# A two-layer decoder trunk on one core: the FFN's down projection by a seven-product scheme, with weight sums made by adding DMA

## The chip, the cores and the metric

The kernel runs on one core of one Trainium2 chip. The metric is the device time of one execution in microseconds (us). Three runs of the kernel before took 1354.49, 1356.29 and 1356.95 us; the median is 1356.29 us.

## The reference, cut to what matters

```python
D_MODEL, SEQ, DEPTH, D_FF = 1024, 512, 2, 2816
def reference(x, ...):
    for l in range(DEPTH):
        proj = x @ w_in[l]
        ...
        mix = jnp.concatenate([o_a, o_b], axis=-1) @ w_out[l]
        x = layer_norm(ALPHA * x + mix, ln1_g[l], ln1_b[l])
        ffn = (jax.nn.silu(x @ w_ffn_gate[l]) * (x @ w_ffn_up[l])) @ w_ffn_down[l]
        x = layer_norm(ALPHA * x + ffn, ln2_g[l], ln2_b[l])
    return x
```

Everything is float32. The change is in the line of `ffn`: three matrix products per layer, 512 x 1024 by 1024 x 2816 twice (gate and up), and 512 x 2816 by 2816 x 1024 (down).

## The kernel before, in words

**Precision.** A float32 product is made of three products in the type fp32r. Each operand is split into a high part (a cast on ScalarE, ACT) and a low part (a subtraction on VectorE, DVE); `mm3` (L78) then issues high x high (L80), low x high and high x low (L81, L82), 128 x 128 stationary elements each, with 256 or 512 moving columns. A weight block of 128 x 1024 comes by DMA from the queue of SyncE (SP) into a raw buffer `wraw`, and is split into `whi` and `wlo` (`load_w`, L53; the cast is L74, the subtraction L75). Raw buffers have the tag `wr` with two buffers, `whi` and `wlo` have three each.

**Gate and up.** The inner layer has 22 blocks of 128 (NF). The first four blocks of gate and of up are plain (`feats`, L176): the first five of these eight products run in two halves of 256 tokens (the list `LEAD2`), the other three with 512 columns. The other 18 blocks go through `seven` (L122), Strassen's scheme in Winograd's form, two blocks (one unit) at a time: seven products of 4 x 3 matmuls with 256 columns each, where plain blocks need eight. Its sums of weights are made in `stage` (L92): `s1` and `s3` are loaded by SP and then added to by a DMA of GpSimd's queue with `accum_op=add` (L100, L101), 128 x 512 elements each. The sums of activations, T1 to T4, are made once per layer (L934 to L942). `seven` computes 18 units per layer.

**Down.** `H[j]`, the hidden block j, is split into high and low (`split_h` L948, `split_rest` L1030). The output has two halves of 512 columns (c = 0, 1) and four tiles of 128 tokens (t). For c = 0, eleven weight blocks (`down_w`, L1051, each 2 x 128 rows by 512 columns) are multiplied for all four t (`wide_mm`, L215); for c = 1 the tiles 0 and 1 come first, then their normalization runs (`norm_turn`, L719, or in the last layer `norm`, L709) beside the products of the tiles 2 and 3. That makes 22 x 4 x 2 x 3 = 528 matmuls of 512 columns per layer. None of the down weights is summed.

**Order.** A scheduler of the framework sets each engine's order when the program is built; every engine and every DMA queue then works in its order. `tc.high_priority(offset)` moves instructions ahead in that order. Buffers are named by tags with a fixed number of buffers; a tile waits until an earlier one of its tag is free.

Of the kernel before, what the change touches and what calls it, by code (L numbers as in the profile page):

```python
# [13 lines left out]
OP = mybir.AluOpType  # L14
# [5 lines left out]
LEAD1 = (("f", 3), None, None, None, ("at", 8))  # L20
LEAD2 = (None, None, ("qs", 6), ("e", 4), ("pt", 4))
# [13 lines left out]
class Kern:  # L35
# [17 lines left out]
    def load_w(self, src, w=1024, tag=None, pieces=1):  # L53
# [5 lines left out]
        if tag is None:  # L59
            hi = [self.sb.tile([128, 1024], F32R, name="whi", tag="wh", bufs=3)]  # L60
            lo = [self.sb.tile([128, 1024], F32R, name="wlo", tag="wl", bufs=3)]
            step = 1024
        elif tag == "a":
            b = self.big("wa", F32R).rearrange("p a b -> p (a b)")
            hi, lo, step = [b[:, :1024]], [b[:, 1024:]], 1024
        else:
            step = w // (1 if tag[0] == "f" else 2)
            hi, lo = ([self.sb.tile([128, 1024 if tag[0] == "f" else 512], F32R, name="wx", tag=tag[0], bufs=tag[1])
                       for _ in range(w // step)] for _ in range(2))
# [52 lines left out]
    def seven(self, units, R):  # L122
# [4 lines left out]
        self.place = 0  # L127
# [8 lines left out]
        for unit in units + [None]:  # L136
# [211 lines left out]
    def hg_levels(self, h, tag):  # L348
# [7 lines left out]
        dg = self.sb.tile([128, 4, 128], F32, name="atd", tag="at", bufs=8)  # L356
        M = self.sb.tile([128, 2, 128], F32, name="atm", tag="a7", bufs=6)
        a7 = self.sb.tile([128, 2, 128], F32, name="at7", tag="a7", bufs=6)
        a8 = self.sb.tile([128, 2, 256], F32, name="at8", tag="at", bufs=8)
# [111 lines left out]
    def take_q(self, u, pt):  # L471
        nc = self.nc
        for i in range(2):
            q = self.sb.tile([128, 512], F32R, name="qs", tag="qs", bufs=6)
# [17 lines left out]
    def compress(self, l, kind, pt, sp):  # L492
# [13 lines left out]
        for half in range(2):  # L506
            for j in range(8):
                if j % 4 == 0:
                    w1 = self.sb.tile([128, 512], F32, name="w1", tag="pt", bufs=4)
                    nc.sync.dma_start(w1, self.io["w1"][l, kind, half][:, j * 128:(j + 4) * 128])  # L510
                nc.tensor.matmul(ph[:, :62], w1[:, j % 4 * 128:(j % 4 + 1) * 128], U[half][:, j].rearrange("p g n -> p (g n)"),
# [67 lines left out]
    def nsa_scores(self, h, b):  # L579
# [7 lines left out]
        e1 = self.sb.tile([128, 512], F32, name="e1", tag="e", bufs=4)  # L587
        e2 = self.sb.tile([128, 256], F32, name="e2", tag="e2", bufs=2)
        e3 = self.sb.tile([128, 512], F32, name="e3", tag="e", bufs=4)
# [37 lines left out]
    def nsa_pv(self, h, b):  # L627
# [6 lines left out]
        for js in ((0,), (1,), (2, 3)):  # L634
# [6 lines left out]
            ph = self.sb.tile([128, 512], F32R, name="pth", tag="pt", bufs=4)  # L641
            pl = self.sb.tile([128, 512], F32R, name="ptl", tag="pt", bufs=4)
# [66 lines left out]
    def norm(self, t, r, p, res):  # L709
# [5 lines left out]
        for c in range(0, 1024, n):  # L715
            nc.vector.scalar_tensor_tensor(r[:, c:c + n], r[:, c:c + n], rs, p[:, 1024 + c:1024 + c + n], op0=OP.mult, op1=OP.add)
            nc.sync.dma_start(res[t * 128:(t + 1) * 128, c:c + n], r[:, c:c + n])
# [35 lines left out]
    def layer(self, l):  # L753
# [44 lines left out]
        if l == 0:  # L798
# [5 lines left out]
              for k0, k1, t in ((0, 3, None), (3, 6, None), (6, 8, ("qs", 6)))]  # L804
# [79 lines left out]
        def second_half():  # L884

            self.stats = [self.small(24, "st", tag="s") for _ in range(NT)]
            self.wo = [self.load_w(io["wo"][l, q, 0], tag=t) for q, t in enumerate((("at", 8), ("at", 8), ("f", 3), None))]
# [56 lines left out]
        NE = 6  # L944
        slots = [self.sb.tile([128, 512], F32R, name="h_" + tag, tag=tag, bufs=n) for tag, n in (("at", 8),) for _ in range(n)]
        H = [None] * NF

        def split_h(j, s):  # L948
            hh, hl = slots[2 * j], slots[2 * j + 1]
            with tc.high_priority(offset=500):  # L950
                nc.scalar.copy(hh, s)
                nc.vector.tensor_tensor(hl, s, hh.bitcast(F32), op=OP.subtract)
            H[j] = [(hh[:, b * 256:(b + 1) * 256], hl[:, b * 256:(b + 1) * 256]) for b in range(2)]

        pend = {}

        def ffn(i, pt):
            if i % 2 == 0:
                s = self.m([128, 512], "silu")
                with tc.high_priority(offset=500):  # L960
                    nc.scalar.activation(s, pt, AF.Silu)
                pend[0] = s
            else:
                s = pend.pop(0)
                with tc.high_priority(offset=500):
                    nc.vector.tensor_tensor(s, pt, s, op=OP.mult)
                split_h(i // 2, s)
# [5 lines left out]
        slots += [self.sb.tile([128, 512], F32R, name="h_pt", tag="pt", bufs=4) for _ in range(4)]  # L973
        raws = {}

        def hidden(j):

            if j < NE:
                return self.m([128, 512], "silu")
            if j - NE < 10:  # L980
                tag, n = (("qs", 6), ("e", 4))[j - NE >= 6]
                return self.sb.tile([128, 512], F32, name="h_" + tag, tag=tag, bufs=n)
            if j % 2 == 0:
                raws["f"] = self.sb.tile([128, 2, 512], F32, name="h_f", tag="f", bufs=3)
            return raws["f"][:, j % 2]

        def gate(j):
            def take(part, acc, add):
                if part == "11":
# [206 lines left out]
```

## Time and profile before

| | |
|---|---|
| runs | 1354.49, 1356.29, 1356.95 us |
| profiled execution | 1357.27 us, span of its instructions 1355.5 us |
| TensorE (PE) busy | 1322.2 us, 98% |
| DVE, ACT, GpSimd (POOL) busy | 938.9, 718.5, 158.6 us |
| granted TensorE clock | 0.996 of full speed |
| DMA | 170.26 MB, mean 126 GB/s |
| FFN of layer 0 | from about 327 us to about 681 us |
| FFN of layer 1 | from about 996 us to about 1344 us |

A matmul row's duration includes its way through a pipeline; the rate is read from the distance of the starts of consecutive rows. The span ends about 1.8 us before the execution's own time does.

### The profile page before, as it was taken

The numbers are of one execution on the slowest core, as the hardware profiler recorded it, in microseconds if no ns is written. First come the engines' busy times: TensorE is split into PE (matmuls) and PEld (weight loads), VectorE is DVE, ScalarE is ACT, GpSimd is POOL, SyncE is SP. The second block draws the span as 40 slices with busy tenths as digits, with TensorE's granted clock in tenths as the row PEclk, the third lists the DMA queues.
The fourth block names the chain that finished last, engine by engine and source line by source line (L and its number), as shares of the span: only waits on it lengthen the run. The fifth ranks groups of instructions, "written<-read, shape, count | busy, mean of one in ns | idle before, by whom it ended". The sixth has DMA issues, their size and how long they took to land.

```text
span 1355.5 us, 23189 instructions
## 1 busy us (share of the span) xinstructions
PE 1322.2 (98%) x8853; PEld 1212.5 (89%) x8853; DVE 938.9 (69%) x1914; ACT 718.5 (53%) x1460; POOL 158.6 (12%) x232
## 2 busy tenths in 40 slices
PE   8999999899999999999999999998999999999996
PEld 6988999789999999888899989987899999998885
DVE  4755898866887777624469468988559777775355
ACT  5254777745565555522543558778265655564131
POOL 1140111110011111000011001111000211100001
PEclk9999999999999999999999999999999999999999
DMA  7252213252177776334534122132513787754344
GB/s 235 79 164 101 78 56 101 55 146 91 63 174 191 180 182 171 102 107 151 191 122 129 65 86 75 55 106 73 154 47 102 181 192 181 181 131 140 94 143 152
DMA packets 61775, 170.26 MB, mean 126 GB/s; under 512 B 7519, under 2 KB 7695, under 8 KB 61152
## 3 DMA queue, kind: packets, MB, share of 16 engines
q1 hardware_dynamic: 44928, 128.93, 29.9%
q0 software_dynamic: 15728, 38.02, 13.4%
q10 hardware_dynamic: 1008, 1.84, 0.4%
q8 instruction: 69, 1.13, 0.3%
q14 instruction: 42, 0.34, 0.1%
HBM read 164.51 MB, written 7.10 MB: 127 GB/s over the span
## 4 chain that ended last, share of the span: by engine, by line
PE 88%; ACT 4%; DMA 3%; DVE 3%; issue 1%; POOL 0%; POOLq 0%; DVEq 0%; ACTq 0%; SPq 0%
PE ps_d L80 16%; PE ps_d L81 15%; PE ps_d L82 15%; PE ps_t L81 4%; PE ps_t L82 4%; PE ps_t L80 4%; PE ps_s L82 4%; PE ps_s L81 4%; PE ps_s L80 4%; PE ps_t L639 2%; DMA wraw<-in_wo 2%; PE ps_h L384 1%; PE ps_o L650 1%; PE ps_o L82 1%; PE ps_o L81 1%; PE ps_o L80 1%
## 5 line engine op out<-in xcount | busy, mean ns | idle before, releaser
L75 DVE TENSOR_TENSOR wlo<-wraw,whi 128x1024 fp32r<-128x1024 f32 (+1 forms) x122 | 149.0, 1221 | 158.2 <-ACT whi L74 157.7
L74 ACT CAST whi<-wraw 128x1024 fp32r<-128x1024 f32 (+1 forms) x122 | 127.5, 1045 | 227.4 <-PE ps_t L82 70.1
L80 PE MATMUL ps_d<-xh,whi 128*128 128x512 f32 (+1 forms) x456 | 154.1, 341 | 3.1 <-ACT gates L490 2.9
L112 ACT CAST whi<-wraw 128x512 fp32r<-128x512 f32 x144 | 89.0, 621 | 124.3 <-PE ps_d L81 93.9
L82 PE MATMUL ps_d<-xh,wlo 128*128 128x512 f32 (+1 forms) x456 | 154.6, 340 | 0.0
L81 PE MATMUL ps_d<-xl,whi 128*128 128x512 f32 (+1 forms) x456 | 154.2, 339 | 0.0
L113 DVE TENSOR_TENSOR wlo<-wraw,whi 128x512 fp32r<-128x512 f32 x144 | 98.4, 689 | 43.4 <-ACT whi L112 39.7
L81 PE MATMUL ps_d<-tl,whi 128*128 128x256 f32 x432 | 121.5, 283 | 0.0
L82 PE MATMUL ps_d<-th,wlo 128*128 128x256 f32 x432 | 120.5, 283 | 0.0
L80 PE MATMUL ps_d<-th,whi 128*128 128x256 f32 x432 | 120.3, 283 | 0.0
L80 PEld LDWEIGHTS ps_d<-xh,whi 128*128 128x128 f32 x456 | 85.8, 190 | 12.3 <-ACT gates L490 3.3
L82 PEld LDWEIGHTS ps_d<-xh,wlo 128*128 128x128 f32 x456 | 86.5, 190 | 8.8
L81 PEld LDWEIGHTS ps_d<-xl,whi 128*128 128x128 f32 x456 | 86.5, 190 | 8.3
L80 PE MATMUL ps_d<-whi,xh 128*128 128x256 f32 (+1 forms) x304 | 90.2, 298 | 0.0
L81 PE MATMUL ps_d<-wlo,xh 128*128 128x256 f32 (+1 forms) x304 | 88.4, 291 | 0.0
L82 PE MATMUL ps_d<-whi,xl 128*128 128x256 f32 (+1 forms) x304 | 87.3, 288 | 0.0
L81 PEld LDWEIGHTS ps_d<-tl,whi 128*128 128x128 f32 x432 | 82.9, 192 | 0.2
L80 PEld LDWEIGHTS ps_d<-th,whi 128*128 128x128 f32 x432 | 82.2, 192 | 0.2
L82 PEld LDWEIGHTS ps_d<-th,wlo 128*128 128x128 f32 x432 | 82.3, 192 | 0.0
L600 ACT ACTIVATE e<-e,mn 128x128 f32<-128x128 f32 (+3 forms) x128 | 71.6, 560 | 13.2 <-DVE mn L598 12.6
L598 DVE CUSTOM_DVE_ANT_0 e<-ps_s,strip 128x128 f32<-128x128 f32 (+3 forms) x128 | 59.2, 484 | 6.8 <-PE ps_s L613 5.9
L643 ACT CAST pth<-ps_t 128x384 fp32r<-128x384 f32 (+1 forms) x96 | 48.8, 510 | 25.9 <-PE ps_t L639 20.8
(482 smaller groups left out, 3957.7 us busy)
## 6 DMA issues: line engine op xcount, KB each, us to landing
wraw<-in_wd SPq DMA_DIRECT2D x59, 512.0 KB, 3.5
wraw<-in_wf SPq DMA_DIRECT2D x31, 512.0 KB, 3.3
wraw<-in_wg SPq DMA_DIRECT2D x26, 512.0 KB, 4.5
wraw<-in_wu SPq DMA_DIRECT2D x26, 512.0 KB, 4.1
ws<-in_wg SPq DMA_DIRECT2D x36, 256.0 KB, 3.5
ws<-in_wg POOLq DMA_DIRECT2D x36, 256.0 KB, 5.2
ws<-in_wu SPq DMA_DIRECT2D x36, 256.0 KB, 3.4
ws<-in_wu POOLq DMA_DIRECT2D x36, 256.0 KB, 4.6
```

The costliest lines, as they stand in the source:

```text
L74: nc.scalar.copy(h, raw[:, i:i + n])
L75: nc.vector.tensor_tensor(o, raw[:, i:i + n], h.bitcast(F32), op=OP.subtract)
L80: first = t.matmul(out, ah, bh, start=start, stop=False, **kw)
L81: t.matmul(out, ah, bl, start=False, stop=False, **kw)
L82: t.matmul(out, al, bh, start=False, stop=stop, **kw)
L112: nc.scalar.copy(h, raw)
L113: nc.vector.tensor_tensor(o, raw, h.bitcast(F32), op=OP.subtract)
L384: nc.tensor.matmul(p2[:, i], S[:, blk(i)], kq(128 * (i + 2), [[2 * w, n], [256 + w, 2], [1, w]]), start=True, stop=True)
L598: nc.vector.tensor_tensor_reduce(out=e, in0=pa, in1=st[:, 512 - pa.shape[-1]:], scale=1.0, scalar=3e38, op0=OP.add, op1=OP.min, accum_out=mn)
L600: nc.scalar.activation(e, e, AF.Exp, bias=mn, scale=-1.0, accum_out=sm)
L639: nc.tensor.transpose(p[:, c:c + 128], E[qt][:, j * 128:(j + 1) * 128], self.ident)
L643: nc.scalar.copy(ph[:, :c], p[:, :c])
```

## The change

It does four things.

1. Gate and up: two blocks each stay plain (all four in two halves of 256 columns, `LEAD2`), and twenty go through `seven` (20 units). Every third unit's raw block goes to the tag `f`. The rest of the first normalization (`norm_rest`) moves behind the third unit.
2. Down: 16 of 22 hidden blocks go through a seven-product scheme, in four groups q of four blocks, in two phases of four groups. In phase 1 a group has four products (called here M, Y, E and Z after their PSUM tiles), 2 x 2 x 3 = 12 matmuls of 512 columns each. M uses the weight block p11 as it is; Y, E and Z use one buffer `s` in which a sum grows: s is loaded by SP and added to once (`raw_w`) for Y, added to again for E, and again for Z. In phase 2 a group has three products (Q with a sum of two blocks, M and N with plain ones), and from the second group on one plain product.
3. The other six hidden blocks stay plain: 72 matmuls of 512 columns for the first tiles and 72 for the others, which come last, beside the normalization of the tiles 0 and 1.
4. Some pairs of 512-column buffers become one of 1024 columns, and in the last layer three of the output's stores go through GpSimd's queue.

The core of the diff (the merging of buffers and the drains into the rows are left out):

```diff
     def stage(self, sa, sb):
...
-            a = self.sb.tile([128, 1024], F32, name="wraw", tag="wr", bufs=2)
+            self.turn += 1
+            tag, bufs = ("f", 3) if self.turn % 3 == 0 else ("wr", 2)
+            a = self.sb.tile([128, 1024], F32, name="wraw", tag=tag, bufs=bufs)
...
-        srcs = [io[w][l, j] for j in range(4) for w in ("wg", "wu")]
-        self.feats(srcs[:5], x1, ffn, LEAD2)
-        self.norm_rest(l, 0, rows, None)
-        self.feats(srcs[5:], x1, lambda i, pt: ffn(i + 5, pt))
...
+        self.feats([io[w][l, j] for j in range(2) for w in ("wg", "wu")], x1, ffn, LEAD2)
...
-        self.seven([(io[w][l, j], io[w][l, j + 1], f(j)) for j in range(4, NF, 2) for w, f in (("wg", gate), ("wu", up))], R)
+        self.seven([(io[w][l, j], io[w][l, j + 1], f(j)) for j in range(2, NF, 2) for w, f in (("wg", gate), ("wu", up))], R,
+                   {3: lambda: self.norm_rest(l, 0, rows, None)})
...
-        for i in range(n):
-            for _ in range(min(len(rest), 4 if i == 0 else 2)):
-                split_rest(rest.pop(0))
-            self.wide_mm(pts, down_w(0, i), hsf, i, i == 0, i == n - 1, i == n - 1)
...
+        def split(dst, src):
+            with tc.high_priority(offset=3000):
+                nc.scalar.copy(dst[0], src)
+                nc.vector.tensor_tensor(dst[1], src, dst[0].bitcast(F32), op=OP.subtract)
...
+        def split_w(raw):
+            w = [self.sb.tile([128, 1024], F32R, name=nm, tag=t, bufs=3) for nm, t in (("whi", "wh"), ("wlo", "wl"))]
+            split(w, raw)
+            return w
+
+        def raw_w(src, plus=None, tag=("wr", 2)):
+            t = self.sb.tile([128, 1024], F32, name="wraw", tag=tag[0], bufs=tag[1])
+            nc.sync.dma_start(t, src)
+            if plus is not None:
+                nc.gpsimd.dma_start(t, plus, accum_op=OP.add)
+            return t
+
+        def dprod(acc, w, r, start, stop):
+            for k in range(2):
+                for t in range(2):
+                    s = slice(t * 128, (t + 1) * 128)
+                    self.mm3(acc[t], r[0][:, k, s], r[1][:, k, s], *(p[:, k * 512:(k + 1) * 512] for p in w),
+                             start and k == 0, stop and k == 1, skip_group_check=True)
...
+        for q in range(QS):
...
+            with tc.high_priority(offset=3000):
+                s = raw_w(wd[1, i], wd[1, i + 1], ("f", 3))
+                p11 = raw_w(wd[0, i])
...
+            dprod(M, split_w(p11), o11, q == 0, False)
+            dprod(Y, split_w(s), o1, q == 0, end)
+            with tc.high_priority(offset=3000):
+                nc.gpsimd.dma_start(s, wd[0, i], accum_op=OP.add)
+            dprod(E, split_w(s), o2, q == 0, end)
+            with tc.high_priority(offset=3000):
+                nc.gpsimd.dma_start(s, wd[0, i + 1], accum_op=OP.add)
+            dprod(Z, split_w(s), o22, q == 0, end)
...
+        for q in range(QS):
...
+            with tc.high_priority(offset=3000):
+                s3 = raw_w(wd[0, i], wd[1, i], ("f", 3))
+                p12, p22 = raw_w(wd[0, i + 1]), raw_w(wd[1, i + 1])
...
+            dprod(Q, split_w(s3), o3, q == 0, end)
+            dprod(M, split_w(p12), o21, False, False)
+            dprod(N, split_w(p22), o4, q == 0, end)
+            if q:
...
+                w1[j] = self.load_w(wd[0, j], tag=("at", 4) if q < 3 else ("pt", 2))
+                plain(M, j, (0, 1), w1[j], False, end)
```

In the changed kernel the cast of `split` is L1015, its subtraction L1016, the load in `raw_w` L1033 and its adding DMA L1035, the two later adding DMAs L1069 and L1072.

**Where the order changes, first place.** ScalarE in the down projection of layer 0, before: casts of down weights (`whi<-wraw`) and of hidden blocks (`hb`).

```order
L74 CAST whi_6448<-wraw_6446 128x1024
L74 CAST whi_6488<-wraw_6486 128x1024
L1039 CAST hb_6555<-h_f_5881 128x256 x2
L1039 CAST hb_6555<-h_f_6134 128x256 x2
L1039 CAST hb_6554<-h_f_6134 128x256
L74 CAST whi_6526<-wraw_6524 128x1024
L74 CAST whi_6566<-wraw_6564 128x1024
L74 CAST whi_6604<-wraw_6602 128x1024
L74 CAST whi_6634<-wraw_6632 128x1024
```

The same engine and place in the changed kernel: `wraw_6316` is s of the first group, `wraw_6403` and `wraw_6400` are p11 and s of the second, the `hop` tiles are operands made of hidden blocks.

```order
L1015 CAST whi_6367<-wraw_6316 128x1024
L1015 CAST hop_6574<-h_qs_5084 128x512
L1015 CAST hop_6678<-h_at_3681 128x512
L1015 CAST hop_6678<-h_at_3824 128x512
L1015 CAST hop_6679<-h_at_3681 128x512
L1015 CAST whi_6384<-wraw_6316 128x1024
L1015 CAST whi_6418<-wraw_6403 128x1024
L1015 CAST whi_6434<-wraw_6400 128x1024
L1015 CAST hop_6743<-h_at_4062 128x512
L1015 CAST hop_6743<-h_at_4325 128x512
L1015 CAST whi_6451<-wraw_6400 128x1024
L1015 CAST hop_6744<-h_at_4062 128x512
```

Before, each cast reads a raw block of its own. Now the casts for E and Z of the first group read the same `wraw_6316` one after the other, and the casts for M and Y of the second group stand behind the one for Z of the first.

**Second place.** GpSimd's queue where `seven` of layer 0 ends, before:

```order
L100 DMA ws1_6058<-in_wg 128x512
L101 DMA ws3_6059<-in_wg 128x512
L100 DMA ws1_6185<-in_wu 128x512
L323 DMA cstrip_8272<-csd_645 128x448
L101 DMA ws3_6186<-in_wu 128x512
L318 DMA strip_8314<-Z_636 128x512
L706 TENSOR_TENSOR rstd_6970<-mv_6967,mhalf_122 128x1
```

and in the changed kernel (`cstrip` and `strip` belong to the next layer):

```order
L102 DMA ws3_6148<-in_wu 128x512
L1069 DMA wraw_6316<-in_wd 128x1024
L325 DMA cstrip_8258<-csd_633 128x448
L320 DMA strip_8300<-Z_624 128x512
L1072 DMA wraw_6316<-in_wd 128x1024
L1069 DMA wraw_6400<-in_wd 128x1024
L1035 DMA wraw_6568<-in_wd 128x1024
L1072 DMA wraw_6400<-in_wd 128x1024
L1069 DMA wraw_6484<-in_wd 128x1024
L1035 DMA wraw_6670<-in_wd 128x1024
L1072 DMA wraw_6484<-in_wd 128x1024
```

Between the last stage of `seven` and the next normalization stand now the adding DMAs of the down weights, group after group. The first adding DMA (L1035) of the first three groups stands earlier, among the stages of `seven`. Layer 1 has the same order in both places, without `cstrip` and `strip`.

## Rows read from the trace of the kernel before

**Rows 1.** The page, part 1: busy us, share of the span, instructions.

```profile
PE 1322.2 (98%) x8853; PEld 1212.5 (89%) x8853; DVE 938.9 (69%) x1914; ACT 718.5 (53%) x1460; POOL 158.6 (12%) x232
```

**Rows 2.** Windows: seven of layer 0, down of layer 0, down of layer 1.

```profile
core 0: us, PE busy (x) PEld busy (x) DVE busy (x) ACT busy (x) POOL busy (x), PEclk, DMA share, GB/s
...
372.00:566.00 194.00, 194.00 (x1568) 191.73 (x1567) 151.61 (x279) 114.67 (x243) 28.61 (x34) 1.00 0.68 169
566.00:696.00 130.00, 128.68 (x634) 108.01 (x633) 56.69 (x72) 44.85 (x53) 7.43 (x7) 1.00 0.46 149
...
1232.00:1344.00 112.00, 112.00 (x498) 92.80 (x497) 47.77 (x54) 29.95 (x32) 3.55 (x3) 1.00 0.44 141
```

**Rows 3.** The page, part 4: the chain that ended last, by engine.

```profile
PE 88%; ACT 4%; DMA 3%; DVE 3%; issue 1%; POOL 0%; POOLq 0%; DVEq 0%; ACTq 0%; SPq 0%
```

**Rows 4.** Timeline of PE in the down projection: start, duration; 512 columns.

```profile
617.64 0.39 PE L80 MATMUL ps_d<-wa,h_at 128*128 128x512 f32 x1
...
619.91 0.39 PE L81 MATMUL ps_d<-wlo,h_at 128*128 128x512 f32 x1
```

**Rows 5.** Timeline of PE in seven: 256 columns.

```profile
377.14 0.28 PE L80 MATMUL ps_s<-xh,whi 128*128 128x256 f32 x1
...
379.31 0.28 PE L80 MATMUL ps_d<-xh,whi 128*128 128x256 f32 x1
```

**Rows 6.** The page, part 5: the splits of a weight block.

```profile
L75 DVE TENSOR_TENSOR wlo<-wraw,whi 128x1024 fp32r<-128x1024 f32 (+1 forms) x122 | 149.0, 1221 | 158.2 <-ACT whi L74 157.7
L74 ACT CAST whi<-wraw 128x1024 fp32r<-128x1024 f32 (+1 forms) x122 | 127.5, 1045 | 227.4 <-PE ps_t L82 70.1 <-DMA wraw<-in_wd 35.8 <-PE ps_d L81 29.0
...
L113 DVE TENSOR_TENSOR wlo<-wraw,whi 128x512 fp32r<-128x512 f32 x144 | 98.4, 689 | 43.4 <-ACT whi L112 39.7
```

**Rows 7.** DMA issues: count, KB each, median us from issue to landing.

```profile
wraw<-in_wd SPq DMA_DIRECT2D x59, 512.0 KB, 3.5
...
ws<-in_wg POOLq DMA_DIRECT2D x36, 256.0 KB, 5.2
...
strip<-Z POOLq DMA_DIRECT2D x16, 256.0 KB, 3.0
```

**Rows 8.** The adding DMAs of L101, all 36 of them: landing times.

```profile
L101 POOL DMA_DIRECT2D ws<-in_wu x18: 843/850/864, 288.6 to 1201.8; - x18
...
DMA to landing us min/median/max: 3.9/4.4/6.7
```

**Rows 9.** The page, part 3: DMA queues, packets, MB, share of 16 engines.

```profile
q1 hardware_dynamic: 44928, 128.93, 29.9%
q0 software_dynamic: 15728, 38.02, 13.4%
```

**Rows 10.** Timeline in seven: a split, and the adding DMA that waits for it.

```profile
451.13 0.69 DVE L113 TENSOR_TENSOR wlo<-wraw,whi 128x512 fp32r<-128x512 f32 x1 [1.50 <-ACT whi L112]
...
452.16 0.85 POOL L101 DMA_DIRECT2D ws<-in_wu  x1 [7.75 <-DVE wlo L113]
```

**Rows 11.** Timeline of DVE, middle of layer 0: last halves of x1, last T sums.

```profile
348.52 0.68 DVE L740 TENSOR_TENSOR xl<-xr,xh 128x512 fp32r<-128x512 f32 x1
...
351.40 2.43 DVE L942 TENSOR_TENSOR tl<-xraw,th 128x1024 fp32r<-128x1024 f32 x2
```

**Rows 12.** The chain, end of layer 0: start us, us, what.

```profile
680.58 0.60 DVE st L1057
...
695.70 0.51 PE ps_d L80 x2
```

**Rows 13.** Windows in layer 0 where PE waited and its clock fell.

```profile
235.00:243.00 8.00, 6.45 (x49) 5.56 (x47) 5.51 (x18) 6.02 (x22) 1.21 (x2) 1.00 0.41 160
243.00:246.50 3.50, 3.50 (x13) 3.25 (x14) 3.29 (x14) 2.08 (x6) 0.61 (x1) 0.51 0.30 80
```

More of the change, by code (lines that the diff above doesn't have):

```diff
@@ L970, in layer @@
[L970 to L985 removed]
+        n = NF // 2
@@ new lines, in add, with stat @@
+        def add(t, half, p, op=OP.add):
+            o = rows[t][:, half]
+            nc.vector.tensor_tensor(o, o, p, op=op)
+        def stat(t, c):
+            nc.vector.bn_stats(self.stats[t][:, c * 6:(c + 1) * 6], rows[t][:, c * 512:(c + 1) * 512])
+        for t in range(2):
+            add(t, two, Q[t], OP.subtract)
+            add(t, two, N[t], OP.subtract)
+            nc.vector.scalar_tensor_tensor(rows[t][:, one], rows[t][:, one], ALPHA, M[t], op0=OP.mult, op1=OP.add)
+            stat(t, 0)
@@ L1068, in layer @@
+        for t in range(2):
+            add(2 + t, two, Q[t], OP.subtract)
         if last:
             lnp = self.ln_params(l, 1)
-        kept = {}
-        pts = {t: self.ps("d") for t in (0, 1)}
-        held = () if last else (0,)
-        for i in range(n):
-            kept[i] = down_w(1, i, "a" if i in held else None)
-            self.wide_mm(pts, kept[i], hsf, i, i == 0, i == n - 1, i == n - 1)
+        js = range(2 * QS, n)
+        pts = {t: self.ps("t") for t in (0, 1)}
+        w2 = {}
@@ L1076, in layer @@
+        for j in js:
+            w2[j] = self.load_w(wd[1, j])
+            plain(pts, j, (0, 1), w2[j], j == js[0], j == js[-1])
         for t in (0, 1):
-            down_end(1, t, pts[t])
+            add(t, two, pts[t])
+            stat(t, 1)
             if last:
@@ L1082, in layer @@
             self.norm_turn(l, 1, 0, rows, self.x)
-        pts = {t: self.ps("oh"[t - 2]) for t in (2, 3)}
-        late = (4, 5, 6, 7) if last else ()
-        order = [*range(n - 3, n), *held, *(i for i in range(n - 3) if i not in held and i not in late)]
-        for j, i in enumerate(order):
-            w = kept[i] if i in held or i >= n - 3 else down_w(1, i)
-            self.wide_mm(pts, w, hsf, i, j == 0, j == n - 1, j == n - 1)
-        for i in late:
-            kept[i] = down_w(1, i, "a")
-        for t in (2, 3):
-            for i in late:
-                self.wide_mm({t: pts[t]}, kept[i], hsf, i, False, i == late[-1])
-            down_end(1, t, pts[t])
-            if last:
-                self.norm(t, rows[t], lnp, io["out"])
+        ends = [{t: self.ps("d") for t in (2, 3)}, {t: self.ps("ho"[t - 2]) for t in (2, 3)}]
+        order = [(ts, c) for ts in ((2,), (3,)) for c in (0, 1)] if last else [((2, 3), 1), ((2, 3), 0)]
+        for ts, c in order:
+            for j in js:
+                plain(ends[c], j, ts, (w1, w2)[c][j], j == js[0], j == js[-1])
+            for t in ts:
+                add(t, (one, two)[c], ends[c][t])
+                stat(t, c)
+                if last and c:
+                    self.norm(t, rows[t], lnp, io["out"])
         if last:
```

179 lines of the change are left out of this document (103 added, 76 removed).

## The prediction

> **What bounds the kernel now.** I read the page's busy times first: the matmul engine (PE) is busy 98% of the span, DVE 69% [rows 1]. The chain of waits says the same, 88% of it is PE [rows 3]. So the next question is whether the changed stages are full too. In the windows, PE is busy for all of 194 us in seven, for 128.68 of 130 us in the down projection of layer 0, and for all of 112 us in that of layer 1 [rows 2]. A stage in which PE never waits gives back every matmul taken out, and has no slack for a wait that is put in. Both follow from the same rows, and the prediction weighs one against the other.
>
> The profiled execution took 1357.27 us (span 1355.5), 0.98 us above the median of the runs shown, 1356.29; the sum is made against 1357.3. A measurement of this kernel tells apart about 0.2%, 2.7 us.
>
> **What the change takes out.** Rates come from starts of consecutive matmuls. Ten intervals from 617.64 to 619.91 us give 0.227 us for 512 columns [rows 4]; 18 intervals from 377.14 to 379.31 us give 0.120 us for 256 [rows 5].
> - Down, per layer: 528 matmuls of 512 columns become, in phase 1, 4 groups x 4 products x 12 = 192, in phase 2 4 x 3 x 12 = 144, and 144 plain ones: 480. 48 x 0.227 = 10.9 us less.
> - Gate and up, per layer. Before: five blocks in halves (48 x 0.120 = 5.8 us each), three whole (24 x 0.227 = 5.4), 18 units of 84 x 0.120 = 10.1 us: 28.8 + 16.3 + 181.4 = 226.5 us. After: four blocks in halves and 20 units: 23.0 + 201.6 = 224.6 us. 1.9 us less.
> - Together 12.8 us per layer, 25.6 us in all. If nothing waits, the time is 1331.7 us.
>
> **What it puts in: a chain through one buffer.** In phase 1 the sum s of a group is split for the product Y, then a DMA adds a block to the same buffer, it is split again for E, another DMA adds, and it is split for Z. The DMA cannot start before DVE has read s, and the split cannot start before the DMA has landed. In the order of ScalarE the casts for M and Y of the next group stand behind the cast for Z of this one, so the groups cannot overlap either, although three buffers s exist. In seven the adding DMAs were issued well ahead, each for a buffer of its own; here eight of them per layer (two in each of four groups) lie in one line with their splits.
>
> The price of a link, d, from the end of the last split to the first cast of the next:
> - Issue: in seven a split ends at 451.82 us and the adding DMA that waits for it starts at 452.16, 0.34 us later [rows 10].
> - Landing: the adding DMAs of 256 KB took 3.9 us at least, 4.4 in the median, 6.7 at most [rows 8]; those of both lines together 5.2 in the median for gate weights [rows 7]. Mine are 512 KB. The queue shares give what the size costs: q1 used 0.299 x 16 x 1355.5 = 6485 us of DMA engines for 128.93 MB, 50 per MB; q0 0.134 x 16 x 1355.5 = 2906 us for 38.02 MB [rows 9]. Of these the 72 adding DMAs are 18.9 MB; with the other 19.1 MB at 50 per MB, adding costs 103 per MB. Another 0.262 MB over 16 engines is then 1.7 us. From the shortest landing, 3.9 + 1.7 = 5.6 us; from the median 6.1.
> - I take 5.6, because the queues are emptier there than in seven (DMA share 0.46 against 0.68 [rows 2]). d = 5.9 us. Bounds: 3.9 + 0.3 = 4.2 if the size costs nothing, 6.7 + 1.7 + 0.3 = 8.7 if every landing is like the slowest.
>
> The other links [rows 6]: a split is 1.05 us on ACT and 1.22 on DVE, 2.3 us for E. From Z's first cast to the next group's Y: 1.05 for the cast, then three subtractions on DVE (Z, M, Y; ACT runs ahead), 3 x 1.22 = 3.7, so 4.7 us. A group therefore takes 2d + 7.0 = 18.8 us, in which PE has 48 x 0.227 = 10.9 us of work.
>
> The whole phase, counted from the end of seven's last product: Y's first split is done 1.7 us later (behind some ten subtractions and additions of 0.69 us [rows 6], of which most run during seven's last two products). Then 8d, four splits for E (9.1), three passages from Z to Y (14.1), one cast for the last Z (1.05), and that product itself (2.7): 8d + 28.7 = 75.9 us. PE's work in it is 15 products of 2.72, 40.8 us (the first M runs before). So PE waits **35.1 us per layer, 70.2 us in all**. At d = 4.2 it is 21.5 per layer, at 8.7 it is 57.5.
>
> **What I cost at nothing, and its cover.**
> - Phase 2: its sums need one adding DMA per group, issued ahead; DVE has 7 to 8 splits and sums of 0.69 and 1.22 us for 10.9 us of PE's work. If a sum is late, one landing, some 6 us.
> - seven: three of the first adding DMAs of s run beside it, on a DMA share of 0.68 [rows 2]; bounded by 0 and one landing each.
> - Middle of a layer: one block less (2.9 us) hides the second half of x1, whose last part was ready at 349.2 us, and the T sums, ready at 353.8 [rows 11]. The four blocks end near 351 us and the products take the T's one after the other in the next 10 us. Between 0 and 3 us per layer; I take 0, since the first products do not use T.
> - End of layer 0: the plain products behind the first half's normalization fall from 11 to 6 (30 to 16.3 us). The second half's chain took 695.70 - 680.58 = 15.1 us [rows 12], so the cover just holds; if it fails, some us once.
> - On GpSimd's queue `cstrip` and `strip` now stand between two adding DMAs; they wait for buffers that DVE has read before the E split, so they add nothing to the chain.
>
> **The sum.** 1357.3 - 25.6 + 70.2 = 1401.9, **1402 us**, 3.3% slower. PE's lost columns are where they were meant to be; the waits take nearly three times as much.
>
> **A rule for the change.** The 512 KB landing of 5.6 us is worked out from rows of 256 KB. By the Trainium skill ("DMA: Bandwidth & Descriptors", Anatomy of one DMA, the gpsimd path), a DMA of that queue takes about 2.0 us plus its bytes over 436 GB/s: an estimate of 3.2 us by that page, with which d would be 3.5 and the time 1364 us (that of the first rival). The trace speaks against it for adding DMAs, since half the size never took under 3.9 us [rows 8].
>
> **Rivals.**
> - *The sums land like plain transfers.* A plain load of 512 KB lands in 3.5 us, and a plain 256 KB on GpSimd's queue in 3.0 [rows 7]. With 3.3, d = 3.6: waits 16.7 per layer, 1357.3 - 25.6 + 33.4 = 1365 us. Against it: the adding rows [rows 8]. Chance 0.07.
> - *Faster: the chain is short enough.* The same chain, with the point from which it decides: 8d - 12.1 = 12.8 gives d = 3.1 us. Below it the change wins, at d = 2 by 18 us, 1340 us, with no waits 1331.7. For it: three buffers s, and PE had no idle time in seven although 72 sums are made the same way [rows 2]. Against it: ScalarE's order, and no adding DMA of even half the size landed that fast. Chance 0.09. Close to the point (within 0.2%) 0.03.
> - *The clock falls too.* PE would wait some 4 us before each E and Z. In layer 0, after 8 us in which PE was busy 6.45, the granted clock was 0.51 for 3.5 us, the lower of its two levels (1.2 instead of 2.4 GHz) [rows 13]. At the lower level all through phase 1, a group's work is 21.8 us against the chain's 18.8: 3 us more per group, and 2.7 for the last product, 12 per layer, 1426 us. Where it falls only after each wait, the slack of the chain hides most of it. By the Trainium skill ("TensorE: Matmul & The Clock Gate", HAM oscillation), waits for DMA between short bursts of matmuls throttle the clock again and again; by that rule 1426 is the time to expect, but the rows show one such fall only. Chance 0.10.
> - *The change does not do what it says*, for instance matmuls that cost more than 0.227 us: the shapes are those of rows 4, so I give it no chance of its own.
>
> **How the numbers follow.** The forecast, 1402 with d between 4.2 and 8.7, has 0.71; its ends are 1357.3 - 25.6 + 43 = 1375 and 1357.3 - 25.6 + 115 = 1447. Slower by over 0.2%: 0.71 + 0.07 + 0.10 = 0.88; same 0.03; faster 0.09. The range for 8 in 10 leaves out the faster cases and most of the rival of plain landings below, and the end of the slow landings above: 1370 to 1430.
>
> **What would show it right or wrong.** In the changed profile: PE busy near 93%; in the two down stages idle time of PE ahead of the hi x hi rows of E and Z, 5 to 6 us each, ended by the ACT cast; ACT's cast of `wraw` waiting for the adding DMA of L1069 and L1072, with landings near 5.6 us; a start-to-start of 18 to 19 us from E to E; no waits of over 1 us in phase 2. Wrong would be: landings of the adding DMAs near 3 us, PE without gaps in phase 1, or idle time that stands elsewhere (before `tl`, or before the plain products at a layer's end).

## The result and the profile after

The changed kernel takes **1413.15 us** (median of 4 runs, 1412.21 to 1413.97), the kernel before in the same session 1355.39 (4 runs, 1354.11 to 1356.95): a ratio of **1.0425, interval 1.0407 to 1.0443**, slower. The forecast was 1402, range 1370 to 1430. The profiled execution took 1413.97 us (span 1412.2), so against the 1331.7 us that the saved columns alone would give, 82.3 us went to waits; the prediction had 70.2.

The page of the changed kernel: part 1, part 4 by engine, the cast of part 5 that stands in the chain, and a line of part 6 (count, KB each, median us from issue to landing).

```profile
PE 1334.7 (95%) x8853; PEld 1211.1 (86%) x8853; DVE 1013.5 (72%) x2005; ACT 748.9 (53%) x1479; POOL 190.9 (14%) x275
PE 53%; DVE 8%; DMA 7%; issue 3%; ACT 2%; POOLq 0%; DVEq 0%; POOL 0%; ACTq 0%
L1015 ACT CAST whi<-wraw 128x1024 fp32r<-128x1024 f32 x56 | 56.9, 1047 | 92.9 <-DMA wraw<-in_wd 81.5
wraw<-in_wd POOLq DMA_DIRECT2D x32, 512.0 KB, 5.8
```

Against [rows 1, 3]: PE's share of the chain falls from 88% to 53%, and a transfer, `wraw<-in_wd`, is now what ScalarE's cast waits for. PE is busy for longer than before although it has fewer columns. The windows explain that: middle of layer 0, seven, phase 1 and the rest of its down projection, then the middle and phase 1 of layer 1.

```profile
core 0: us, PE busy (x) PEld busy (x) DVE busy (x) ACT busy (x) POOL busy (x), PEclk, DMA share, GB/s
325.00:372.00 47.00, 43.38 (x348) 41.67 (x347) 35.73 (x53) 30.95 (x53) 5.48 (x7) 0.99 0.41 118
372.00:562.80 190.80, 190.68 (x1568) 189.82 (x1568) 153.75 (x274) 109.51 (x222) 30.11 (x35) 0.99 0.70 176
562.80:642.70 79.90, 55.93 (x189) 40.26 (x188) 41.58 (x51) 27.04 (x35) 11.30 (x14) 0.85 0.60 129
642.70:708.00 65.30, 65.22 (x292) 53.52 (x291) 42.51 (x54) 28.32 (x31) 2.00 (x4) 1.00 0.55 168
...
1021.00:1067.00 46.00, 42.15 (x343) 40.72 (x343) 34.58 (x52) 31.13 (x53) 5.50 (x7) 1.00 0.42 120
...
1259.10:1338.60 79.50, 57.65 (x189) 40.94 (x188) 41.39 (x51) 26.99 (x35) 9.37 (x11) 0.83 0.57 122
```

Phase 1 has 189 matmuls in the window, at 0.227 us [rows 4] 42.9 us of work, in 79.9 and 79.5 us: 37.0 and 36.6 us lost. PE counts as busy for 55.93 of them because the granted clock was 0.85 on average, and a matmul at the lower clock is busy for longer (0.63 us at 573.05, 0.39 at the full clock). The middle of a layer loses 3.6 and 3.9 us. Together 81.1, near the 82.3. Seven and phase 2 lose 0.12 and 0.08 us by their busy time.

Not all of the 3.6 and 3.9 is the change's: 1.3 us of each are a wait of the first normalization's transposes (327.22 and 1023.08 us), which the kernel before has too (1.2 us, at 326.04 and 995.19). In exchange the busy time of seven hides that behind the middle the granted clock fell:

```profile
370.70:374.30 3.60, 3.48 (x18) 3.19 (x17) 3.60 (x6) 1.31 (x3) 0.00 (x0) 0.53 0.21 63
```

18 matmuls of 256 columns, 2.2 us of work at 0.120 us [rows 5], took 3.5: some 1.3 us more. So what the change costs here per layer is about 2.3 to 2.6 us of waits and 1.3 of slow matmuls.

The chain of waits through layer 0's phase 1 (start us, us, what; the longest pieces) shows the line that the prediction drew, a landing, the splits, a landing (the 2.60 us of "issue" are the split for E):

```profile
572.71 5.59 DMA wraw<-in_wd
580.53 2.37 DVE wlo L1016 x2
583.19 5.81 DMA wraw<-in_wd
589.06 2.60 issue
591.67 5.09 DMA wraw<-in_wd
599.05 2.37 DVE wlo L1016 x2
...
611.25 5.11 DMA wraw<-in_wd
...
630.14 5.18 DMA wraw<-in_wd
```

The links for Z (the second adding DMA) start at 572.71, 591.67, 611.25 and 630.14: a group of layer 0 takes 19.0, 19.6 and 18.9 us. From the end of the split at 582.90 (580.53 + 2.37) to the DMA at 583.19 are 0.29 us.

### The profile page after: what moved, and what is told of

The parts are those of the page before. It is cut to its first block, busy times and chain, and to the rows that moved or that the text cites. A ratio compares the mean times of both kernels' runs of the same rounds, so it can differ in the third digit from the quotient of the medians.

```text
span 1412.2 us, 23417 instructions
## 1 busy us (share of the span) xinstructions
PE 1334.7 (95%) x8853; PEld 1211.1 (86%) x8853; DVE 1013.5 (72%) x2005; ACT 748.9 (53%) x1479; POOL 190.9 (14%) x275
## 4 chain that ended last, share of the span: by engine, by line
PE 53%; DVE 8%; DMA 7%; issue 3%; ACT 2%; POOLq 0%; DVEq 0%; POOL 0%; ACTq 0%
PE ps_d L79 9%; PE ps_d L80 9%; PE ps_d L81 9%; DMA wraw<-in_wd 6%; PE ps_t L81 3%; PE ps_t L80 3%; PE ps_t L79 3%; PE ps_s L80 2%; DVE wlo L1016 2%; PE ps_s L81 2%; PE ps_s L79 2%; ACT whi L1015 1%; PE ps_t L644 1%; DVE hop L1016 1%; PE ps_h L387 1%
## 5 line engine op out<-in xcount | busy, mean ns | idle before, releaser
L79 PE MATMUL ps_d<-xh,whi 128*128 128x256 f32 (+1 forms) x424 | 141.0, 336 | 1.6 <-ACT gates L494 1.1
L81 PE MATMUL ps_d<-xh,wlo 128*128 128x256 f32 (+1 forms) x424 | 142.4, 336 | 0.0
L80 PE MATMUL ps_d<-xl,whi 128*128 128x256 f32 (+1 forms) x424 | 141.0, 333 | 0.8 <-DVE mv L709 0.8
L81 PE MATMUL ps_d<-th,wlo 128*128 128x256 f32 x480 | 134.4, 285 | 1.6 <-DVE wlo L114 1.6
L80 PE MATMUL ps_d<-tl,whi 128*128 128x256 f32 x480 | 135.8, 285 | 0.0
L79 PE MATMUL ps_d<-th,whi 128*128 128x256 f32 x480 | 134.7, 285 | 0.0
L73 ACT CAST whi<-wraw 128x1024 fp32r<-128x1024 f32 (+1 forms) x68 | 70.7, 1040 | 97.4 <-PE ps_d L80 19.4
L1016 DVE TENSOR_TENSOR wlo<-wraw,whi 128x1024 fp32r<-128x1024 f32 x56 | 67.3, 1222 | 72.7 <-ACT whi L1015 72.6
L74 DVE TENSOR_TENSOR wlo<-wraw,whi 128x1024 fp32r<-128x1024 f32 (+1 forms) x68 | 82.3, 1211 | 50.4 <-ACT whi L73 50.2
L1015 ACT CAST whi<-wraw 128x1024 fp32r<-128x1024 f32 x56 | 56.9, 1047 | 92.9 <-DMA wraw<-in_wd 81.5
```

Of the source, the lines that this page charges most:

```text
L73: nc.scalar.copy(h, raw[:, i:i + n])
L74: nc.vector.tensor_tensor(o, raw[:, i:i + n], h.bitcast(F32), op=OP.subtract)
L79: first = t.matmul(out, ah, bh, start=start, stop=False, **kw)
L80: t.matmul(out, ah, bl, start=False, stop=False, **kw)
L81: t.matmul(out, al, bh, start=False, stop=stop, **kw)
L1015: nc.scalar.copy(dst[0], src)
```

## The experiments

Times of one session are compared through the kernel before, which ran with each (medians of 1354.61 to 1357.67). "At 1355.4" is the ratio times 1355.4.

| kernel | median us | ratio to before, interval | at 1355.4 |
|---|---|---|---|
| changed | 1413.15 | 1.0425 [1.0407, 1.0443] | 1413.0 |
| no links | 1339.68 | 0.989 [0.9871, 0.991] | 1340.5 |
| one link | 1379.09 | 1.0188 [1.0164, 1.0213] | 1380.9 |
| plain links | 1390.66 | 1.0267 [1.0242, 1.0293] | 1391.6 |
| pipelined | 1350.47 | 0.9963 [0.9945, 0.9981] | 1350.4 |
| second order | 1350.05 | 0.9966 [0.9948, 0.9984] | 1350.8 |
| plain down | 1356.33 | 1.0015 [1.0002, 1.0028] | 1357.4 |
| DVE sums | 1361.32 | 1.0041 [1.0024, 1.0058] | 1361.0 |
| second order, no residual scale | 1339.28 | 0.9884 [0.9866, 0.9905] | 1339.7 |
| second order, spread | 1346.87 | 0.9919 [0.9898, 0.9939] | 1344.4 |
| first order, spread | 1344.91 | 0.991 [0.9893, 0.9926] | 1343.2 |
| changed, spread | 1412.39 | 1.04 [1.038, 1.0421] | 1409.6 |
| one link, shared split | 1368.4 | 1.0092 [1.0056, 1.0129] | 1367.9 |

### No links

```diff
-                nc.gpsimd.dma_start(s, wd[0, i], accum_op=OP.add)
...
-                nc.gpsimd.dma_start(s, wd[0, i + 1], accum_op=OP.add)
```

> Both later adding DMAs of phase 1 (for E and for Z) are left out, so E and Z use the same weights as Y and two thirds of the growing sum is missing from the result; every matmul, split and load stays. Chain theory (the eight landings per layer that lie in one line with their splits cost what the kernel lost): no link is left, PE's 40.8 us of phase 1 cover the splits, and the time falls by some 77 us from 1413, to 1331.7 plus about 4 us for the waits seen in the middle of each layer, 1336 us (1331 to 1345). Rival, the split load (two engines have more splits and sums per matmul in phase 1 than they can make): the splits all stay, so it would fall by less than a third of that and stay above 1390. Rival, the seams (gate and up, the start of phase 1, the layer's end): the same, above 1390.

Ratio 0.989: 72.5 us less than the changed kernel, with every split, load and matmul still there. The window from seven's end to phase 2, at the full clock:

```profile
559.40:602.70 43.30, 42.30 (x185) 33.99 (x184) 36.12 (x44) 26.25 (x34) 4.53 (x6) 1.00 0.58 146
```

43 us where the changed kernel needs 80, and 1340.5 lies in the expected range. The split load, the rival, is excluded as the main cause; so are the seams.

### One link

```diff
-                nc.gpsimd.dma_start(s, wd[0, i + 1], accum_op=OP.add)
```

> Only the last adding DMA of each group (for Z) is left out, so Z uses the weights of E and one summand is missing from the result. Chain theory: four links per layer instead of eight; a group takes d + 7.0 = 12.9 us against 10.9 of PE's work; waits 4d - 12.1 = 11 us per layer, so 1336 + 23 = about 1359 us (1350 to 1368), and the start-to-start from E to E falls from 19 us to about 13. If instead each link cost the same share (half of 77 us), 1374. Rival, split load or seams: above 1400.

A miss: 1380.9, not 1359; half the links keep 56% of the loss. ScalarE's timeline over one group (start us, us, engine, line, operation; what it waited for):

```profile
582.44 2.94 ACT L1015 CAST whi<-wraw 128x1024 fp32r<-128x1024 f32 x3 [4.50 <-DMA wraw<-in_wd]
...
588.92 1.05 ACT L1015 CAST whi<-wraw 128x1024 fp32r<-128x1024 f32 x1 [3.02 <-PE ps_d L81]
...
597.93 2.94 ACT L1015 CAST whi<-wraw 128x1024 fp32r<-128x1024 f32 x3 [5.24 <-DMA wraw<-in_wd]
```

From 582.44 to 597.93 is 15.5 us. The landings, 6.2 us in the median, would make d + 7.0 13.5. The three casts for E, Z and the next M take all three buffers `whi`; the cast for the next Y, at 588.92, waits until PE has finished E's product (`ps_d`), and only after it can the next link start. With one link PE's product joins the line, which d + 7.0 does not contain.

### Plain links

```diff
-                nc.gpsimd.dma_start(s, wd[0, i], accum_op=OP.add)
+                nc.gpsimd.dma_start(s, wd[0, i])
...
-                nc.gpsimd.dma_start(s, wd[0, i + 1], accum_op=OP.add)
+                nc.gpsimd.dma_start(s, wd[0, i + 1])
```

> The two later DMAs of each group stay on the same queue, with the same size and the same waits, but overwrite s instead of adding to it, so E and Z use single blocks in place of sums. It separates the chain from the price of adding. With the price of a plain landing, 3.0 to 3.5 us in place of 5.2 to 5.8: d = 3.6, waits 8d - 12.1 = 17 us per layer instead of some 38, 1336 + 33 = 1369 us (1360 to 1380). If adding itself costs nothing and the landing is long for its 512 KB or its place on that queue, the landings stay above 5 us and the time above 1405. If every link under 3.1 us hides, the time is within 2 us of the kernel without links.

1391.6, not 1369. The two lines' landings, first for the plain links, then for the adding ones of the changed kernel:

```profile
L1069 POOL DMA_DIRECT2D wraw<-in_wd x8: 527/529/557, 562.6 to 1295.7; - x8
DMA to landing us min/median/max: 3.9/4.4/5.2
...
L1072 POOL DMA_DIRECT2D wraw<-in_wd x8: 533/543/546, 569.9 to 1303.1; - x8
DMA to landing us min/median/max: 3.7/3.8/3.8
```

```profile
L1069 POOL DMA_DIRECT2D wraw<-in_wd x8: 847/855/857, 564.8 to 1315.9; - x8
...
DMA to landing us min/median/max: 5.2/5.8/7.2
...
L1072 POOL DMA_DIRECT2D wraw<-in_wd x8: 845/847/884, 572.7 to 1325.8; - x8
...
DMA to landing us min/median/max: 5.1/5.2/5.6
```

With adding, the landing of 512 KB takes 1.4 us longer on both lines. The plain landing was taken too short: 4.1 us on average of the two medians, not 3.3. With it, d = 4.1 + 0.34 = 4.4, and 8d - 12.1 = 23.1 us per layer on top of the kernel without links gives 1340.5 + 46.2 = 1387, near the 1391.6 measured. So the linear sum holds for two links per group, and a plain transfer in that line would have lost too.

### The pipelined order

```diff
-        for q in range(QS):
...
-            dprod(M, split_w(p11), o11, q == 0, False)
-            dprod(Y, split_w(s), o1, q == 0, end)
...
+        for x in "M0 Y0 M1 Y1 Y2 Y3 E0 M2 E1 E2 E3 Z0 Z1 Z2 Z3 M3".split():
+            step(x[0], int(x[1]))
```

> The whole computation, with the same 16 products, sums and adding DMAs in phase 1, in another order: Y of all four groups, then E of all four, then Z of all four, with three of the M between and the fourth M last, and four sums in flight (the fourth in a raw buffer). Four products (10.9 us) stand between a group's Y and its E, and between its E and its Z, against a link of 5.9 us and a split of 2.3. Chain theory: all eight landings hide, about 1337 us (1332 to 1348), faster than the kernel before the change. Rivals: the price is the DMAs' or the splits' volume, not their line, then it stays above 1395; four adding DMAs at a time slow each other to twice their landing, then some 3 us per product are left, 1360 to 1375.

Ratio 0.9963: faster than the kernel before, 62.6 us less than the changed kernel, with the same transfers and splits in another order (and the fourth sum in another buffer). That is 2.4 us above the expected range, and far below both rivals. The landings did slow each other, as the second rival said (median 7.4 us, up to 9.4), yet four products cover them:

```profile
L1070 POOL DMA_DIRECT2D wraw<-in_wd x16: 838/850/1027, 561.1 to 1246.3; - x16
...
DMA to landing us min/median/max: 5.1/7.4/9.4
```

```profile
556.00:600.00 44.00, 43.22 (x195) 35.39 (x194) 34.10 (x43) 25.44 (x34) 10.47 (x13) 1.00 0.92 219
600.00:613.00 13.00, 10.48 (x40) 6.81 (x39) 11.34 (x16) 7.75 (x10) 1.70 (x2) 1.00 0.87 212
```

Phase 1 loses 0.8 us; the passage to phase 2, 600 to 613, loses 2.5. There the cast of phase 2's first sum (600.58) stands 5.05 us until its adding DMA, issued at 594.74, has landed, and M's next product waits 1.06 us for the drain.

### A second order

The same with `"M0 Y0 M1 Y1 M2 M3 Y2 E0 Y3 E1 E2 Z0 E3 Z1 Z2 Z3"`, and the fourth sum in the raw buffer after the four `p11`.

> The whole computation, with a second order of the 16 products of phase 1: all M stand early (M0 Y0 M1 Y1 M2 M3 Y2 E0 Y3 E1 E2 Z0 E3 Z1 Z2 Z3), so that M, Y and E are complete, and can be drained, while PE still works on Z, and the first sum of phase 2 finds its buffer free earlier. With the first order the passage from phase 1 to phase 2 cost some 4 us per layer (a first split of phase 2 that waited for its adding DMA, and a product that waited for the drain). If that is the cause, 1350.5 - 8 = 1342 us (1337 to 1347). Rival: landings of 7.5 us in place of 5.5, because several adding DMAs run at once, set the time of both orders; then three products between a group's sums hide less than four do, and it is 1350 us or more.

The rival's time, 1350.8, but not its cause: the landings were shorter than in the first order (6.2 us in the median). The passage is gone, but another wait came: one of 4.9 us for the cast before Y3, in PE's waits from 575 to 600 us:

```profile
PE ps_s L79 <- ACT whi L1015: 4.9, 1, 4.9
```

The fourth sum shares its buffer with M's raw blocks, so it is loaded and added to later: its first adding DMA is issued at 573.77 us, in the first order at 559.67.

### The change without Strassen in down

The loops of both phases are replaced by eleven plain pairs of blocks, eight into all eight PSUM tiles and three at the layer's end:

```diff
+        for j in range(2 * QS):
+            hs(j)
+            for c in range(2):
+                plain(acc[c], j, range(NT), self.load_w(wd[c, j]), j == 0, False)
```

> The whole computation with gate and up, their buffers and the layer's end as changed, and the down projection plain for all 22 blocks (528 matmuls of 512 columns): the change without its Strassen part. The gate-and-up part saves 1.9 us per layer by its columns, and the waits in the middle of a layer cost about 2.7: 1355.2 - 3.8 + 5.4 = 1357 us (1352 to 1363), no difference from before that can be told. Then the loss of 58 us is the down projection's alone, and its Strassen part without later sums (1339.7) is worth 17 to 18 us. Rival: the seams (middle of the layer, a shorter cover at the layer's end) cost more than 10 us, then it is above 1365.

As expected, 1357.4: 0.15% above before, which is no loss that matters. So 1413.0 - 1357.4 = 55.6 of the changed kernel's 57.6 us are the down projection's, and its Strassen part without links is worth 1357.4 - 1340.5 = 16.9 us, of 21.8 by columns.

### Sums by DVE

```diff
-                nc.gpsimd.dma_start(s, wd[0, i], accum_op=OP.add)
+                nc.vector.tensor_tensor(s, s, p11, op=OP.add)
...
-                nc.gpsimd.dma_start(s, wd[0, i + 1], accum_op=OP.add)
+                p12 = raw_w(wd[0, i + 1])
+                nc.vector.tensor_tensor(s, s, p12, op=OP.add)
```

> The whole computation in the order of the changed kernel, but the two later sums of a group are made by DVE (two additions of 128x1024, some 1.22 us each, with one more plain load) in place of adding DMAs. The line through s stays, each link shrinks from about 5.9 us to 1.3. DVE then has four weight splits, six hop splits and sums and two additions, 4 x 1.22 + 6 x 0.69 + 2 x 1.22 = 11.5 us per group, against 10.9 of PE's work. Chain theory: near the kernel without links, 1340 plus 0.6 per group, 1345 us (1338 to 1356). Rival, DVE's load decides in phase 1: 1370 or more.

Between the two, and outside the expected range: 1361.0, so 52 of the 72.5 us come back without any change of order. The first 14 us of phase 1, and 54 us from its start:

```profile
562.00:576.00 14.00, 8.30 (x31) 5.87 (x30) 14.00 (x21) 7.30 (x11) 1.12 (x2) 0.88 0.30 85
562.00:616.00 54.00, 47.66 (x201) 37.47 (x200) 48.49 (x56) 28.72 (x38) 4.56 (x6) 0.97 0.61 166
```

DVE is busy for all of the first 14 us (it prepares the activations of later groups ahead of the sums), and PE loses 5.7 of its 6.3 us there. I read this as a line that is short enough and a load at the start that is not; no run separates the two.

### The middle of a layer

`norm_rest`, which the change moves behind the third unit, puts eight DVE operations of 128x1024 there. DVE's timeline in the changed kernel, then PE's:

```profile
362.25 4.62 DVE L753 TENSOR_TENSOR r<-r,lnp 128x1024 f32<-128x1024 f32 x4
...
368.33 1.21 DVE L754 TENSOR_TENSOR r<-r,lnp 128x1024 f32<-128x1024 f32 x1
369.46 0.68 DVE L114 TENSOR_TENSOR wlo<-wraw,whi 128x512 fp32r<-128x512 f32 x1
```

```profile
368.76 0.38 PE L79 MATMUL ps_t<-xh,whi 128*128 128x256 f32 x1 [0.87 <-ACT whi L113]
...
370.20 0.39 PE L81 MATMUL ps_d<-th,wlo 128*128 128x256 f32 x1 [0.70 <-DVE wlo L114]
```

PE has used up the weights that were split ahead when DVE comes back to them. These two waits, 1.6 us, are the part of the 3.6 us that stands at the eight operations (in layer 1 they are 1.16 and 0.91). Left out, on the second order:

```diff
-                   {3: lambda: self.norm_rest(l, 0, rows, None)})
+                   {})
```

> As the second order of phase 1, without the eight operations of DVE that apply the first normalization's scale and shift to the residual (they stand, four in one stretch of 4.6 us, ahead of weight splits in the third unit of gate and up), so the residual of the inner layer is wrong by that. If those operations are the middle-of-layer waits, the waits vanish and it takes 2.7 us per layer less than with them, 1342 - 5 = 1337 us. Rival, the T sums are late (what the prediction named): they stay in place, and the time is the same within 1 us.

1339.7, 11.1 us less than the second order, more than expected. In its profile PE loses 0.46 and 0 us in the middle windows, where the second order's lost 2.18 and 2.32; the second order's wait of 4.9 us was missing as well (0.5 us at most), although the landings were not shorter, and why is open. So the place is shown, the 11 us are not its price. Spread over the units 5 to 12, one operation behind each unit's splits:

```diff
+                   {i + 4: lambda i=i: self.norm_step(l, 0, rows, i) for i in range(8)})
```

> The whole computation: the second order of phase 1, and the eight scale and shift operations of the residual put one by one behind the weight splits of the units 5 to 12 (an order dependency on DVE), where seven's splits are some products ahead. If the middle-of-layer waits came from their standing together ahead of the splits of the third unit, nearly all that leaving them out gained comes back: 1341 us (1337 to 1346), about 1% faster than the kernel before. If DVE's volume was the cause, it stays at 1348 to 1352.

> The same spreading with the first order of phase 1 (all Y, all E, all Z). Its profile showed some 4 us per layer lost at the passage to phase 2, the second order's a wait of 5 us for one sum in one layer; by these, 1350.5 - 6 = 1344 us (1340 to 1349), within 4 us of the second order.

1344.4 and **1343.2**, 6.4 and 7.2 us below the same orders without it, and 0.9% (0.991, 0.9893 to 0.9926) below the kernel before: the fastest kernel of the whole computation in this study, though its interval overlaps that of the other. The second order gets back 6.4 of the 11.1 us, not nearly all; its trace has a wait before a Y again (3.9 us). The stretch of the third unit in both layers, first in the changed kernel, then in the first order with spreading (1014 to 1031 is the same place as 1050 to 1067):

```profile
355.00:372.00 17.00, 15.42 (x122) 14.87 (x120) 16.91 (x25) 9.66 (x20) 3.15 (x4) 0.97 0.72 203
1050.00:1067.00 17.00, 14.93 (x123) 14.55 (x122) 16.89 (x25) 11.07 (x22) 3.18 (x4) 1.00 0.79 223
...
355.00:372.00 17.00, 17.00 (x144) 17.00 (x143) 14.07 (x25) 10.65 (x23) 2.59 (x3) 1.00 0.87 249
1014.00:1031.00 17.00, 17.00 (x144) 17.00 (x143) 15.00 (x26) 12.27 (x25) 3.19 (x4) 1.00 0.83 238
```

The waits of 1.6 and 2.1 us are gone, and so is the lower clock behind them.

The same edit on the changed kernel itself:

> The whole computation, the changed kernel with its one-line chain in phase 1, and only the eight operations of the residual spread over the units 5 to 12. It prices the middle-of-layer term inside the changed kernel, where PE lost about 2.1 us there per layer, and the granted clock fell once per layer behind it: 1413 - 5 = 1408 us (1405 to 1411). If the T sums were the cause, or if the start of phase 1 swallows the gain, 1412 to 1414.

Not settled by the time: the ratio falls by 0.0025 (3.4 us), the intervals overlap. In the trace the middles give back 2 us each, and phase 1 of layer 0 begins 3.85 us earlier (558.95 for 562.80), 1.0 of which stands ahead of the middle; phase 1 takes most of it again:

```profile
558.95:641.75 82.80, 58.44 (x189) 41.58 (x188) 40.85 (x50) 27.02 (x35) 10.53 (x13) 0.84 0.57 121
...
1253.50:1337.80 84.30, 60.01 (x191) 42.27 (x190) 41.40 (x52) 26.95 (x35) 9.39 (x11) 0.82 0.55 113
```

```profile
L1078 POOL DMA_DIRECT2D wraw<-in_wd x8: 850/857/859, 561.0 to 1315.0; - x8
...
DMA to landing us min/median/max: 5.4/7.0/7.9
```

82.8 and 84.3 us in place of 79.9 and 79.5: the links for E (L1078 here) landed in 7.0 us in the median, 5.8 in the changed kernel. Why they did is open. So that the spreading is worth 6 to 7 us is shown only where phase 1 is not one line.

### One link, one split less

```diff
-            dprod(E, split_w(s), o2, q == 0, end)
+            es = split_w(s)
+            dprod(E, es, o2, q == 0, end)
...
-            dprod(Z, split_w(s), o22, q == 0, end)
+            dprod(Z, es, o22, q == 0, end)
```

> As the kernel with one link per group (the last adding DMA left out, so that one summand is missing for Z), and Z uses E's split weights, which are the same values: one split less per group, and so one of the three split buffers less. It tests why the one-link kernel took 15.5 us per group where d + 7.0 gave 13 to 14: there ScalarE's cast for the next Y waited for PE to end E's product, because M, E and Z held all three split buffers. If that is the cause, a group is 6.3 + 0.34 for the link and 1.05 + 3 x 1.22 for the splits, 11.4 us, close to PE's 10.9, and the time is 1355 us (1346 to 1364), of which the missing split itself explains 1.22 us per group, 10 us in all. If the link or its landing under load is longer than taken, a group stays above 14 us and the time above 1368.

1367.9, 13.0 us below the one-link kernel: more than the 10 of the missing split, less than the 26 expected. Its landings were long, a median of 7.4 us, which puts a group at 12.5 in place of 11.4. In layer 0's trace the four links start 13.1 us apart on average (563.7 to 603.1), in the one-link kernel 15.1 (560.9 to 606.2). That three full split buffers lengthened the one-link line is shown by the row at 588.92; how much of the 13 us was theirs is not.

## Why the prediction was right

- **The columns.** 25.6 us: not seen directly. Without links the kernel comes to 1340.5, 8.8 above 1331.7, and its trace has 2.6 and 3.0 us of idle PE in the middles, 1.0 and 0.7 in phase 1.
- **The link.** Landing 5.6 us: measured 5.8 for E and 5.2 for Z in the median, 5.5 together; issue 0.34: 0.29. The rate for adding, from the shares of two queues [rows 9], gave 1.7 us for the step from 256 to 512 KB; the shortest landings of the two sizes in the changed kernel are 3.6 and 5.1, a step of 1.5. That the sum began from the shortest landing had some luck in it. The 3.9 us are those of one line; the other adding line before, L100, has 5.7 in the median, and 5.7 + 1.7 would have been 7.4. The reason given, emptier queues (0.46), held in part: the DMA share of phase 1 was 0.60 and 0.57. The Trainium skill's formula ("DMA: Bandwidth & Descriptors", Anatomy of one DMA) gave 3.2 us for this size; no adding DMA of 512 KB landed under 5.0 here, and even the plain ones of that queue took 3.7.
- **The group.** 18.8 us against 19.0, 19.6, 18.9.
- **The phase.** 75.9 us and 35.1 of waits per layer. From the end of seven's last product to that of the last Z are 79.3 us (562.92 to 642.26) and 79.0 (1259.24 to 1338.21). The start was as forecast: Y's first split is done at 564.50, 1.6 us later (1.7). The three groups take 57.4 us against 56.4 in layer 0. What was mis-sized is the last product, 2.7 us in the sum and 5.8 and 6.1 here:

```profile
636.49:642.26 5.77, 5.55 (x16) 3.93 (x17) 5.17 (x6) 1.84 (x2) 0.36 (x1) 0.70 0.53 136
1332.16:1338.21 6.05, 5.82 (x16) 3.94 (x17) 6.03 (x8) 1.85 (x2) 0.00 (x0) 0.72 0.38 109
```

  Four matmuls of phase 2 stand among its twelve (0.9 us), and the granted clock was 0.51 from 637.1 to 640.6 in layer 0.
- **The middle of a layer**, costed at nothing with bounds of 0 to 3 us. This is the term that failed: 3.6 and 3.9 us in the windows, of which 1.3 each stand in the kernel before, and some 1.3 of slow matmuls behind them. The reason was wrong as well. No wait of PE there is for a T sum; the step that the prediction left out is the eight DVE operations of `norm_rest`, moved ahead of weight splits. With 73.6 for the phases and 7.5 here, the sum is 1357.3 - 25.6 + 81.1 = 1412.8; that it meets the time so closely is in part luck, since the 7.5 holds the 2.6 that is not the change's and lacks the slow matmuls.
- **Phase 2 and seven at nothing.** Right by the busy time: 0.08 and 0.12 us lost in layer 0, 0.71 and 0.04 in layer 1.
- **What would show it.** Waits of 5 to 6 us ahead of E and Z were not seen, nor do they fit the prediction's own sum: 35.1 us over eight products are 4.4 each. In the waits of PE from 562 to 643 us the four ahead of Z are 4.0 at most, those ahead of E 4.1 once and little after:

```profile
PE ps_t L79 <- ACT whi L1015: 14.8, 4, 4.0
PE ps_d L79 <- ACT whi L1015: 6.0, 4, 4.1
```

  and PE was busy 95%, not 93%. The rest of the loss stands as slow matmuls.
- **The clock rival.** What it names happened, and did not decide. Windows around the first links of layer 0, waits and low clock by turns:

```profile
575.70:579.10 3.40, 0.82 (x4) 0.34 (x2) 0.00 (x0) 0.79 (x1) 0.00 (x0) 1.00 0.52 100
579.10:582.60 3.50, 3.19 (x7) 2.32 (x8) 3.21 (x3) 2.15 (x3) 0.00 (x0) 0.51 0.20 51
582.60:596.10 13.50, 10.10 (x42) 7.36 (x40) 3.41 (x5) 2.71 (x4) 2.55 (x3) 1.00 0.82 180
596.10:603.10 7.00, 5.17 (x12) 3.89 (x13) 3.50 (x3) 2.94 (x3) 0.86 (x2) 0.51 0.40 119
```

  After 3.4 us with four matmuls the granted clock is 0.51 (1.2 GHz), then full again, then 0.51. Only some of the phase runs at the lower level (0.85 on average), and there PE would have waited for the next link anyway, so 1413 and not the rival's 1426. In the last product, behind which no link stands, the low clock did cost time: 2.1 and 2.4 us, near the rival's 2.7 for it. The Trainium skill ("TensorE: Matmul & The Clock Gate", HAM oscillation) has waits for DMA between bursts of matmuls throttle the clock again and again; the trace agrees, with 0.51 in both windows behind a wait. No run here holds the clock up with the links in one line.
- **The other rivals.** Plain landings: a link as in the third experiment, 36 us over before, so that rival's 1365 was also too low. Faster: shown possible with the order changed, not with the line as written.

## What to carry to other kernels

A sum that grows in place turns transfers into a line: count its links, and compare links plus splits with the matmul work of one turn, not with the bandwidth. Independent accumulators allow another order; putting other groups' products between the steps of one sum gave back 62.6 of the 72.5 us that the links cost, with no byte less. And when a change moves elementwise work, look for what stands behind it in that engine's order, and not only at the operations that the change is about.

## What was not expected of the hardware

- A landing of an adding DMA of 512 KB is not one number. In the changed kernel the links to Z took 5.1 to 5.6 us and the first link to E of each layer 5.2. The other six links to E took 5.7 to 7.2; behind each of them another adding DMA (L1035) was issued 1.4 to 1.9 us later. With several at once it was 5.1 to 9.4 in the first order, up to 10.0 with spreading and 10.6 in the kernel without the residual's operations. The hiding distance has to fit the upper end.
- In the pipelined order PE lost 2.5 of 13 us at the passage and the granted clock stayed at 1.00. In the changed kernel 3.4 us with 0.82 of work were followed by 0.51, but so were 4.7 us with 3.12 of work in the middle of layer 0 (366.0 to 370.7) by 0.53, and the 3.6 us at that clock cost nearly as much as the waits themselves.
